# Graph message passing by sorting edges: smaller last copies in the sort's rotations, a split activation behind it, other zero matmuls ahead of it

## The chip, the cores and the metric

The kernel runs on one NeuronCore of a Trainium2 chip. The metric is the device time of one execution in microseconds (us); lower is better. Engines are named as in the profile: PE (matrix engine; PEld is its weight load), DVE (vector engine), ACT (scalar engine), POOL and SP (here mostly queues that issue transfers). A line number such as L1104 is a line of the kernel file before the change.

## The reference

There are N = 4096 nodes with D = 256 features and E = 262144 edges with random ends.

```python
self_out = nodes @ w_self
src_feat = nodes[edges_src]
msg = src_feat @ w_msg
agg = np.zeros((N, D), dtype=np.float32)
np.add.at(agg, edges_dst, msg)
return (self_out + agg).astype(np.float32)
```

## The kernel before

The kernel sorts the edges and then turns gather and scatter into dense matmuls. The order of instructions on every engine is written out by hand (`tc.manual_schedule()`), so each engine works its list strictly in the order of the program, and waits are placed by the data.

**Keys and the first sort.** Source and destination of each edge become one fp32 key in `XA` (128 partitions, 2048 columns). `_Sort.run` (L1109) walks over the list `SORT_A`. Entries 'b' are compare passes along the columns (a min and a max by DVE, all recorded at line L974). Entries 'q' are rotations: `rotate` (L1091) turns each column by its own number of partitions. There are eight rotations here, which the texts call the first to the eighth. The block `bb` of their columns is 32, 16, 8, 2, 2, 2, 1 and 2: in the seventh neighbouring columns belong to different turns, and a copy writes with a stride of 8 columns.

**A rotation** has two halves of 1024 columns. For each half PE multiplies eight groups of 128 columns by shifted identity matrices (fp32 matmuls, each recorded twice, so a half has 16 records at L1100). Four groups fill one PSUM tile `tp_sw` of 512 columns, of which there are four (`bufs=4`), and ACT copies each tile back to the other one of the two `XA` buffers (L1104), so a half has two copies.

**What lies between rotations.** `near` (L1028) does the passes up to the next rotation in waves: first what needs only the first half of the columns, then what completes the first half, then the second half. So PE can turn the first half while DVE still works on the second, and DVE can begin the next passes on the turned first half while PE turns the second.

**Zero matmuls.** `keep_warm(n)` (L991) issues n matmuls of zeros (128x512, tile `warm`, L994). `warm` (L978) places them ahead of a rotation's first half: for each number in `spans` it goes back that many us over DVE's compare operations, by estimated durations, and makes n zero matmuls wait for the operation found there. `WARM` (L48) lists spans and n for the eight rotations and the place behind the last of them. They stand in PE's list behind the second half of the rotation before, and ahead of the next rotation's matmuls. `FILLS` (L49) says how much of the dense work on the nodes (L321, L325) stands behind each rotation; behind the fourth, sixth and seventh there is none.

**Behind the rotations.** `relayout` (L1149) transposes the keys into `XS` and `XR`, `tail` (L1168) finishes the sort of the first half of the edges, with zero matmuls of its own ahead of its end. Then 16 fp32 matmuls (L453) and 16 more that subtract each chunk's base (L462) fill two PSUM tiles. ACT turns each tile into `vals` (int16, 1024 columns) with one Relu activation of 512 columns (L467): column 8q + k of `vals` comes from column 128k + q of the tiles, so any run of 8 columns needs both tiles. `split_vals` (L529) reads the first 32 columns of `vals` first (L536, L537), then columns 32 to 151, and so on.

**The main part.** For each of 2048 chunks of 128 edges, DVE and ACT build one-hot matrices (L579, L564, L592, L601), PE counts them into a ring in PSUM (L628), ACT moves finished runs to `atr` (L655), and PE multiplies those with the projected nodes `Y` (L718, L725). Group after group of chunks goes through two sets of one-hot buffers.

## Time and profile before

| | |
|---|---|
| median of 3 runs | 419.08 us (418.66 to 419.38) |
| the profiled execution | 418.17 us |
| its span, first to last instruction | 416.4 us |
| mean granted clock of PE over the span | 0.978 of full speed |
| busy: PE, DVE, ACT, POOL | 335.5, 374.9, 270.0, 43.0 us |

The span is split by the profile into work of engines and waits between them; 418.17 - 416.4 = 1.77 us of the profiled time lie outside it. The sort fills the span up to about 154 us, the main part the rest. [...] A row of the timeline merges like instructions in a row; its first number is the start, its second the time from the first start to the last end, and in brackets stands how long the engine sat idle before and what released it.

### The profile page before, as it was taken

Reading aid. Unit: us, or ns where it says so; the run is one execution under the profiler, and the core shown is the slowest. Engines: PE = TensorE matmul, PEld = TensorE weight load, DVE = VectorE, ACT = ScalarE, POOL = GpSimd, SP = SyncE. Lnnn points to the kernel's source line nnn. Section 1 sums busy time; section 2 is a strip of 40 time slices with the busy share of each in tenths; the row PEclk is TensorE's granted clock in tenths of the full one; section 3 lists DMA queues with packets and bytes.
Section 4 is the critical chain, followed back from the end, with each engine's and each line's share of the span. In section 5 each row is a group of like instructions: output and inputs, shape, how many; then the busy total and the mean of one; then the engine's idle time right before and its main releaser. Section 6 shows DMA issues by size and latency. Waiting matters only on the chain.

```text
span 416.4 us, 10756 instructions
## 1 busy us (share of the span) xinstructions
PE 335.5 (81%) x4128; PEld 287.9 (69%) x4137; DVE 374.9 (90%) x916; ACT 270.0 (65%) x559; POOL 43.0 (10%) x172
## 2 busy tenths in 40 slices
PE   0038477876967198999999998898988999999995
PEld 0025255564845056999999998797878988898895
DVE  6999999999799989999999999989997999998851
ACT  4328154553538015889888888996876877777782
POOL 8400000000000000002011020100102030202010
PEclk9999699999999689999999999999999999999999
DMA  8690000101023200003012020230203020211212
GB/s 305 138 185 4 2 1 2 50 0 52 1 101 116 87 0 2 2 2 39 2 16 28 2 32 10 53 41 8 33 3 39 2 32 12 28 14 15 29 16 53
DMA packets 18074, 16.20 MB, mean 39 GB/s; under 512 B 3684, under 2 KB 16997, under 8 KB 18022
## 3 DMA queue, kind: packets, MB, share of 16 engines
q0 software_dynamic: 8992, 6.29, 12.7%
q1 hardware_dynamic: 8310, 7.20, 5.3%
q10 hardware_dynamic: 720, 2.00, 1.2%
q8 instruction: 34, 0.56, 0.6%
q14 instruction: 18, 0.15, 0.1%
HBM read 8.93 MB, written 8.66 MB: 42 GB/s over the span
## 4 chain that ended last, share of the span: by engine, by line
DVE 47%; PE 45%; issue 3%; ACT 3%; DMA 1%; DVEq 0%; ACTq 0%
DVE XA L974 18%; PE out_ps L718 18%; PE ring L628 17%; DVE e_oh L601 7%; PE tp_sw L1100 5%; DVE d_oh L601 5%; DVE XS L974 4%; DVE XR L974 3%; DVE off L564 3%; PE warm L994 2%; PE out_ps L725 1%; DMA d<-in_edges_dst_dram 1%; ACT XA L1104 1%; DVE atr L688 1%; ACT atr L655 1%
## 5 line engine op out<-in xcount | busy, mean ns | idle before, releaser
L655 ACT CAST atr<-ring 128x472 bf16<-128x472 f32 (+11 forms) x352 | 177.2, 553 | 45.7 <-PE ring L628 40.7
L718 PE MATMUL out_ps<-Y,atr 128*128 128x256 bf16 x1024 | 162.2, 272 | 2.9 <-DVE atr L688 2.0
L628 PE MATMUL ring<-d_oh,e_oh 128*128 128x88 bf16 (+9 forms) x2048 | 149.7, 203 | 9.9 <-issue 4.5
L628 PEld LDWEIGHTS <-e_oh 128*128 128x128 bf16 x2048 | 129.2, 97 | 16.4 <-issue 9.7
L718 PEld LDWEIGHTS <-atr 128*128 128x128 bf16 x1024 | 90.7, 97 | 10.8 <-DVE atr L688 2.3
L974 DVE TENSOR_TENSOR XA<-XA 128x510 f32<-128x510 f32 (+30 forms) x154 | 89.3, 630 | 6.9 <-ACT XA L1104 5.3
L601 DVE TENSOR_SCALAR e_oh<-off 128x1024 bf16<-128x1024 int16 (+5 forms) x254 | 87.0, 402 | 7.9 <-PE ring L628 5.2
L628 PE MATMUL ring<-zer 128*128 128x158 bf16 (+12 forms) x352 | 81.4, 231 | 0.1
L866 POOL DMA_DIRECT2D out_dram<-o_sb x30 | 28.9, 963 | 357.8 <-ACT atr L655 357.8
L601 DVE TENSOR_SCALAR d_oh<-off 128x1024 bf16<-128x1024 int16 (+5 forms) x204 | 63.9, 373 | 0.0
L1104 ACT COPY XA<-tp_sw 128x512 f32<-128x512 f32 x32 | 20.9, 654 | 41.5 <-PE tp_sw L1100 41.2
L1100 PE MATMUL tp_sw<-XA,id 128*128 128x128 f32 x256 | 36.7, 298 | 7.9 <-DVE XA L974 7.8
L1100 PEld LDWEIGHTS tp_sw<-XA,id 128*128 128x128 f32 x256 | 33.1, 194 | 13.7 <-DVE XA L974 8.7
L564 DVE TENSOR_TENSOR off<-pair,rows 128x2048 int16<-128x2048 int16 (+5 forms) x34 | 38.6, 1134 | 0.3
L628 PEld LDWEIGHTS <-zer 128*128 128x128 bf16 x352 | 34.1, 97 | 5.0 <-ACT atr L655 1.9
L994 PE MATMUL warm<-zw 128*128 128x512 bf16 x61 | 20.8, 440 | 17.5 <-DVE XS L974 9.3
L349 PE MATMUL x_ps<-id_bf,nodes_bf 128*128 128x128 bf16 x64 | 8.5, 304 | 29.3 <-DMA nodes_bf<-in_nodes_dram 28.0
L725 PE MATMUL out_ps<-Y,atr 128*88 128x256 bf16 (+7 forms) x115 | 31.2, 272 | 0.0
L688 DVE TENSOR_TENSOR atr<-atr 128x178 bf16<-128x178 bf16 (+24 forms) x100 | 23.7, 260 | 6.4 <-ACT atr L655 6.0
L349 PEld LDWEIGHTS <-nodes_bf 128*128 128x128 bf16 x64 | 6.6, 139 | 30.9 <-DMA nodes_bf<-in_nodes_dram 28.3
L321 PE MATMUL y_ps<-wcat,XT 128*128 128x256 bf16 x128 | 21.7, 278 | 6.9 <-ACT Y L325 2.8
L592 ACT ACTIVATE e_oh<-off,onesc 128x512 bf16<-128x512 uint16 (+5 forms) x36 | 24.6, 686 | 2.7 <-DVE off L564 2.7
(114 smaller groups left out, 223.3 us busy)
## 6 DMA issues: line engine op xcount, KB each, us to landing
out_dram<-o_sb POOLq DMA_DIRECT2D x30, 128.0 KB, 3.2
nodes_bf<-in_nodes_dram POOLq DMA_DIRECT2D x2, 1024.0 KB, 12.6
out_dram<-nodes_bf SPq DMA_DIRECT2D x4, 512.0 KB, 2.9
out_dram<-XA SPq DMA_DIRECT2D x4, 512.0 KB, 3.0
d<-in_edges_dst_dram SPq DMA_DIRECT2D x2, 512.0 KB, 5.5
s<-in_edges_src_dram ACTq DMA_DIRECT2D x2, 512.0 KB, 5.7
d<-in_edges_dst_dram SPq DMA_DIRECT2D x1, 480.0 KB, 9.6
s<-in_edges_src_dram ACTq DMA_DIRECT2D x1, 480.0 KB
```

Source lines behind the costliest of these rows:

```text
L564: tt(out=v[:, 0:n // 2].rearrange("p g w (k i) -> p (g w) k i", i=2), in0=pair[:, g].rearrange("p g w i -> p (g w) i").unsqueeze(2).to_bro ...
L601: ins = tss(out=o[:, 0:n // 2, j:j + m].rearrange("p g k i -> p g (k i)"), in_=v[:, 0:n // 2, w, 0:2 * m], scalar=float((-j0 if w else ON_ ...
L628: mm = nc.tensor.matmul(out=ap, lhsT=lhsT, rhs=rhs, start=start, stop=True, skip_group_check=True,).ins
L655: ins = nc.scalar.copy(out=at[:, 0:n], in_=ring[:, b:b + n]).ins
L688: tt(out=atr[:, j:j + n, 0:m], in0=atr[:, j:j + n, 0:m], in1=atr[:, i:i + n, at:at + m], op=ALU.add,)
L718: nc.tensor.matmul(out=out_ps[:, i, :], lhsT=at[:, t * P:(t + 1) * P], rhs=Y[:, b, :], start=(b == 0 and not last and t % 2 == 0), stop=(b ...
L725: nc.tensor.matmul(out=out_ps[0:m, 0, :], lhsT=spill[:, c0:c0 + m], rhs=Y[:, b, :], start=False, stop=False, skip_group_check=True,)
L866: nc.gpsimd.dma_start(out=dst, in_=src, accum_op=ALU.add).ins,
L974: self.nc.vector.tensor_tensor(out=out, in0=in0, in1=in1, op=op),
L994: self.nc.tensor.matmul(out=w[:], lhsT=self.zw[:, 0:P], rhs=self.zw[:], start=True, stop=True).ins
L1100: self.nc.tensor.matmul(out=tp[:, g * P:(g + 1) * P], lhsT=self.turned(rots[8 * h + 4 * t + g]), rhs=sel(x)[:, 4 * t + g], start=True, sto ...
L1104: self.nc.scalar.copy(out=sel(y)[:, 4 * t:4 * t + 4], in_=tp[:].rearrange("p (g i b) -> p g i b", g=4, b=bb),)
```

## The change

1. `rotate` fills and copies three PSUM tiles per half: one of four groups (512 columns) and two of two groups (256 columns). The matmuls are the same; a rotation has 6 copies where it had 4, and 6 tiles of the four `tp` buffers.
2. `vals` is written by four activations where there were two: first the columns 0 to 31 from each of the two tiles (16 elements per partition each), then the rest from each (496 elements). All four stand behind the matmuls of both tiles.
3. `WARM` is changed. Ahead of the first rotation there are five sets of three zero matmuls, at 6.0, 4.8, 3.6, 2.4 and 1.2 us, where there were two sets at 2.7 and 1.4. Ahead of the fifth, seventh and eighth rotation there are two sets of three (2.7 and 1.4), where there was one (1.6). The others keep two sets at 2.7 and 1.4.

```diff
-WARM = [((2.7, 1.4), 3)] * 4 + [((1.6,), 3), ((2.7, 1.4), 3), ((1.6,), 3), ((1.6,), 3), ((2.7, 1.4), 3)]
+WARM = [((6.0, 4.8, 3.6, 2.4, 1.2), 3)] + [((2.7, 1.4), 3)] * 8
+TURNED = ((0, 4), (4, 2), (6, 2))
...
-        nc.scalar.activation(
-            out=vals[:].rearrange("p (q k) -> p q k", k=GP)[:, :, 4 * t:4 * t + 4],
-            in_=tp[:].rearrange("p (k q) -> p q k", k=4),
-            func=ACTF.Relu, scale=-1.0, bias=top[:],
-        )
+    for q in (slice(0, 32 // GP), slice(32 // GP, P)):
+        for t, tp in enumerate(tps):
+            nc.scalar.activation(
+                out=vals[:].rearrange("p (q k) -> p q k", k=GP)[:, q, 4 * t:4 * t + 4],
+                in_=tp[:].rearrange("p (k q) -> p q k", k=4)[:, q],
+                func=ACTF.Relu, scale=-1.0, bias=top[:],
+            )
...
-            for t in range(2):
-                tp = self.psum.tile([P, 512], FP32, name="tp_sw", tag="tp", bufs=4)
-                for g in range(4):
+            for g0, n in TURNED:
+                tp = self.psum.tile([P, 512], FP32, name="tp_sw", tag="tp", bufs=4)[:, 0:n * P]
+                for g in range(n):
                     self.nc.tensor.matmul(
-                        out=tp[:, g * P:(g + 1) * P], lhsT=self.turned(rots[8 * h + 4 * t + g]),
-                        rhs=sel(x)[:, 4 * t + g], start=True, stop=True,
+                        out=tp[:, g * P:(g + 1) * P], lhsT=self.turned(rots[8 * h + g0 + g]),
+                        rhs=sel(x)[:, g0 + g], start=True, stop=True,
                     )
                 self.nc.scalar.copy(
-                    out=sel(y)[:, 4 * t:4 * t + 4],
-                    in_=tp[:].rearrange("p (g i b) -> p g i b", g=4, b=bb),
+                    out=sel(y)[:, g0:g0 + n],
+                    in_=tp.rearrange("p (g i b) -> p g i b", g=n, b=bb),
                 )
```

## Rows read from the trace of the kernel before

**Rows 1.** The page: granted clock in 40 slices; share of the chain by engine.

```profile
PEclk9999699999999689999999999999999999999999
...
DVE 47%; PE 45%; issue 3%; ACT 3%; DMA 1%; DVEq 0%; ACTq 0%
```

**Rows 2.** The chain in order of time: start, us, what; first and second rotation.

```profile
49.63 2.29 PE tp_sw L1100 x16
...
60.63 2.07 PE tp_sw L1100 x16
```

**Rows 3.** Timeline of DVE, 52 to 126 us: compare passes behind the rotations.

```profile
52.57 10.52 DVE L974 TENSOR_TENSOR XA<-XA 128x511 f32<-128x511 f32 x16 [0.66 <-ACT XA L1104]
63.34 10.49 DVE L974 TENSOR_TENSOR XA<-XA 128x511 f32<-128x511 f32 x16 [0.25 <-ACT XA L1104]
...
93.12 7.84 DVE L974 TENSOR_TENSOR XA<-XA 128x515 f32<-128x515 f32 x12 [0.26 <-ACT XA L1104]
...
109.09 3.03 DVE L974 TENSOR_TENSOR XA<-XA 128x510 f32<-128x510 f32 x8 [2.28 <-ACT XA L1104]
112.82 5.14 DVE L974 TENSOR_TENSOR XA<-XA 128x510 f32<-128x510 f32 x8 [0.70 <-ACT XA L1104]
118.33 7.84 DVE L974 TENSOR_TENSOR XA<-XA 128x514 f32<-128x514 f32 x12 [0.36 <-ACT XA L1104]
```

**Rows 4.** Timeline of ACT at the second rotation.

```profile
62.72 0.59 ACT L1104 COPY XA<-tp_sw 128x512 f32<-128x512 f32 x1 [0.31 <-PE tp_sw L1100]
...
65.23 0.59 ACT L1104 COPY XA<-tp_sw 128x512 f32<-128x512 f32 x1 [0.31 <-PE tp_sw L1100]
65.71 0.66 ACT L325 CAST Y<-y_ps 128x256 bf16<-128x256 f32 x2
```

**Rows 5.** Instruction groups of ACT by shape: count, busy us, mean ns, idle before.

```profile
L325 ACT COPY XA<-y_ps 128x256 f32<-128x256 f32 x16 | 5.2, 380 | 1.5 <-PE y_ps L321 1.5
...
L498 ACT ACTIVATE rel_q<-XR,g7f 128x128 int16<-128x128 f32 x8 | 2.9, 404 | 0.0
...
L519 ACT ACTIVATION_READ_ACCUMULATOR XR<-vals,limit 128x1 f32 x1 | 0.2, 192 | 0.0
```

**Rows 6.** The tile tp_sw: shortest, median and longest ns of its copies.

```profile
L1104 ACT COPY XA<-tp_sw x32: 586/590/1107, 51.1 to 117.7; 128x512 f32<-128x512 f32 x32
```

**Rows 7.** Timeline of PE: zero matmuls ahead of the first rotation and in the tail.

```profile
47.08 2.56 PE L994 MATMUL warm<-zw 128*128 128x512 bf16 x5 [5.32 <-DVE XA L974]
...
144.51 5.12 PE L994 MATMUL warm<-zw 128*128 128x512 bf16 x11 [9.25 <-DVE XS L974]
```

**Rows 8.** Windows: stretch, length, busy of five engines, granted clock, DMA.

```profile
50.00:50.50 0.50, 0.50 (x5) 0.50 (x4) 0.50 (x2) 0.00 (x0) 0.00 (x0) 0.70 0.00 0
...
149.25:149.50 0.25, 0.25 (x3) 0.23 (x2) 0.25 (x1) 0.00 (x0) 0.00 (x0) 0.93 0.00 0
```

**Rows 9.** Timeline of PE ahead of the fifth, seventh and eighth rotation.

```profile
86.42 0.81 PE L994 MATMUL warm<-zw 128*128 128x512 bf16 x3
87.47 0.99 PE L1100 MATMUL tp_sw<-XA,id 128*128 128x128 f32 x6 [0.24 <-DVE XA L974]
...
102.91 0.81 PE L994 MATMUL warm<-zw 128*128 128x512 bf16 x3
104.01 0.91 PE L1100 MATMUL tp_sw<-XA,id 128*128 128x128 f32 x3 [0.30 <-DVE XA L974]
...
111.48 0.83 PE L994 MATMUL warm<-zw 128*128 128x512 bf16 x2
112.15 0.72 PE L1100 MATMUL tp_sw<-XA,id 128*128 128x128 f32 x5
```

**Rows 10.** Timeline at the end of the sort: the activations of vals, its first reader.

```profile
153.12 1.52 ACT L467 ACTIVATE vals<-tp_sw,top 128x512 int16<-128x512 f32 x2 [17.45 <-PE tp_sw L462]
...
154.67 0.18 DVE L536 TENSOR_SCALAR pair<-vals 128x32 int16<-128x32 int16 x1 [1.09 <-ACT vals L467]
```

**Rows 11.** Timeline of PE at the third group of chunks.

```profile
162.69 0.28 PE L628 MATMUL ring<-d_oh,e_oh 128*128 128x88 bf16 x3 [1.10 <-DVE d_oh L601]
```

## The prediction

> **What bounds the kernel now.** I began with the page. Its chain of waits is almost all DVE and PE [rows 1], so an edit counts only where it moves the point at which one of them hands over to the other. Next I read that chain in order of time through the sort. It goes from DVE to PE and back at every rotation: DVE's passes, 16 records of PE that turn a half, one copy by ACT, then DVE again [rows 2]. The timeline of DVE shows what each handover costs: DVE sits idle for a copy behind every rotation, 0.66 us at the first, 0.25 at the second (the third and fourth are like it, 0.24 each), 0.26 at the fifth, 2.28 and 0.70 at the seventh, 0.36 at the eighth [rows 3]. Behind 118.33 no further idle of DVE for a copy stands in that group; DVE runs on into the tail, and the next place that the change touches is `vals`, for which DVE waits 1.09 us [rows 10]. A gain is passed on where nothing else is late, and it can be no larger than the idle that it eats. That is the method: handover by handover.

> **Smaller last copies.** A copy of 512 columns takes 0.590 us [rows 6], one of 256 columns 0.380 [rows 5]. So the last copy of a half ends 0.21 us sooner, if ACT is free when PE has finished the last two groups. There are three copies in a row now. The gap between the first and the last copy of a half is 0.59 + 0.31 = 0.90 us [rows 4]; ACT must fit the first copy and the middle one into it. Without overlap that is 0.59 + 0.38 = 0.97, 0.07 too much, and with the pauses between instructions the gain is only about 0.1. But a copy at 65.23 that lasts 0.59 is followed by another at 65.71, 0.48 after its start [rows 4], and two of 256 columns take 0.66 together, not 0.76. With overlap the first two need 0.48 + 0.28 = 0.76 us, and the last starts as soon as PE is done. I take 0.21 and keep 0.1 as the other bound. In the seventh rotation the copy writes with a stride and takes 1.107 us [rows 6]; with the fixed part that 0.590 and 0.380 imply (0.17 us) half of its columns take 0.17 + 0.94 / 2 = 0.64, a gain of 0.47. The other bound is a plain half, 0.55.

> The PSUM tiles cost nothing: the fifth and sixth tile of a rotation reuse the buffers of its first and second, whose copies end before PE turns the second half's second tile, a half (2.07 us) later. If that cover were gone, PE would wait up to one copy, 0.59.

> **The first rotation.** Ahead of it PE had been idle for 5.32 us, and six zero matmuls (five recorded) took 2.56 us, 0.43 each [rows 7], which is the pace of 1.2 GHz; the clock came up inside the slice 50.0 to 50.5 (0.70 there [rows 8], so at 50.3). The half ended at 49.63 + 2.29 = 51.92, though DVE had released it before 49.5. At full clock a half takes 2.07 [rows 2] and would end at about 51.5, 0.4 sooner. The new zeros start some 6 us ahead of the half, near 43.4. In the two places where rows show the clock rise it took 50.3 - 47.08 = 3.2 us, and in the tail 149.3 - 144.51 = 4.8 us, of zeros [rows 7, 8]; either brings it to 2.4 GHz before 49.5. The sets come 1.2 us apart and three zeros take 1.28 us even at the low clock, so they do not pile up into the rotation. With the smaller copy 0.4 + 0.21 = 0.61 of the 0.66 us idle goes. DVE then needs the turned second half one wave (2.57 us, half of 5.14 [rows 3]) later, at about 54.5; PE starts that half at 51.91 and its copy ends at 51.91 + 2.07 + 0.02 + 0.38 = 54.4. So it just fits.

> **Second and third rotation.** 0.21 of 0.25 us each, 0.42 together. The second half's copy also ends 0.21 sooner, so no new wait takes its place.

> **Fourth and fifth, with three more zeros.** The fourth gives 0.21. But the zeros ahead of the fifth stand behind the fourth's second half on PE, and the rotation behind them. Three zeros push the eighth rotation from 111.48 to 112.15, so one costs 0.22 at full clock [rows 9]; six take 1.34. The fifth rotation then starts at 86.42 + 1.34 = 87.76, not 87.47, and its first half is copied at 87.76 + 2.07 + 0.02 + 0.38 = 90.23. DVE, which reached that point at 93.12 - 0.26 - 2.57 = 90.29, would now be there at 90.08 and waits. It continues at 90.25, ends its wave at 92.82, when the second half's copy is there, and not at 93.12. The two rotations give 0.30 in place of 0.42 or more.

> **Sixth to eighth.** Six zeros behind the sixth's second half: the seventh starts at 102.91 + 1.34 = 104.25, not 104.01, which uses up the sixth's gain and 0.24 more. PE turns both halves of the seventh without a pause, so its last copy ends 0.24 later and 0.47 sooner: DVE goes on at 112.59, not 112.82. Then the eighth: three more zeros (0.67) and the delay (0.24) put its first half at 113.06, its copy at 113.06 + 2.07 + 0.02 + 0.38 = 115.53, and DVE, ready at 112.59 + 2.57 = 115.16, waits until 115.55, one wave before 118.12. Before, that was 118.33: 0.21 are left of what the copies alone would give (0.21 + 0.47 + 0.21 = 0.89).

> **The values.** DVE's first read needs both tiles. Before, it waited for the second activation of 512 columns, from about 153.95 to 154.65 [rows 10]. Now it waits for one of 16 columns. The nearest rows are 0.404 us for 128 columns with a bias and 0.192 for a single column [rows 5]; I take 0.30. So DVE starts at 153.95 + 0.30 + 0.02 = 154.27, 0.40 sooner (bounds 0.29 and 0.51). The two long activations run on to about 155.5, and nothing but the read of columns 32 to 151, some 4 us later, needs them. At the third group of chunks PE waits 1.10 us for DVE's one-hots [rows 11], so PE takes over the whole shift there, and I see nothing in the main part tied to absolute time.

> [...]

> **Sum.** 0.61 + 0.42 + 0.30 + 0.21 + 0.40 = 1.94 us. Against its own time the profiled execution would come to 418.17 - 1.94 = 416.23 us. The median of the runs is 0.91 above that execution, and all three runs are. Carried along unchanged that gives 417.14. But part of the 0.91 can be the clock. Had it risen at the first rotation 4.8 us after the first zero, as in the tail, it would have risen at 51.9, 1.6 us later; at half speed that costs PE 0.8 us, all on the chain. The early zeros remove that in every execution. I split the difference and put the forecast at 416.6 us.

> [...]

> **Rivals.**
> (a) The copies do not overlap: 0.1 in place of 0.21 at seven handovers, about 0.5 less in all: 417.1. For it speaks that waits on PE lie between them; against it the row at 65.71.
> (b) The clock takes some back, or the runs' 0.91 us has another cause. The tail's zeros are unchanged and the rise came there at 149.3, just in time for its matmuls. Shifted by 1.6 us it would cost 0.8: 417.4, and 417.9 if the 0.91 stays too.
> (c) The gain is hidden: DVE finds the second half's copy late, so that only the first rotation's clock (0.4) and the values (0.4) count: 419.08 - 0.8 = 418.3, or 417.8 with half of the 0.91. Margins of 0.1 us at the first rotations speak for it.
> (d) Slower: the added zeros become the bound. At 0.43 each, six take 2.56. The fifth rotation starts 1.5 late and loses about 1.2. The seventh starts at 105.47, 1.46 late, and the eighth at 111.48 + 1.46 + 2.56 = 115.50, 3.35 late against a slack of 0.9: 2.5 lost. Against 1.43 gained elsewhere this is 2.3 slower, 420.9 counted from where the forecast starts (418.6). It decides from a clock of about 1.2 GHz between 84 and 118 us; the slices show 9 there throughout [rows 1].

> **How the numbers follow.** The forecast has 0.55 (its own range 416.0 to 417.2), (a) 0.15, (b) 0.14, (c) 0.08, (d) 0.04; 0.04 remain for no change. Leaving out the upper part of (b) and (c), (d), no change and the tails of the forecast, the range is 415.6 to 417.7. About 0.2% (0.84 us) is what a measurement of this kernel can tell from no change. Faster by more takes the forecast, (a), (b) and most of (c), 0.91; within it 0.05; slower 0.04.

> **What the profile of the changed kernel would show.** Granted clock 1.0 in the whole first rotation. DVE's idle below 0.1 us at the first four rotations; copies of about 0.38 us, the last of a half starting with no ACT work ahead of it. Six zeros directly in front of the fifth, seventh and eighth rotation, with no idle of PE, and DVE idle 0.2 and 0.4 us where it now waits for their first halves. DVE's first read of `vals` about 0.4 us behind the last L462 matmul. I am wrong if ACT's three copies stand end to end, if DVE's idle only moves to second halves, or if the clock falls ahead of a rotation.

## The result, and the profile after

The changed kernel takes 412.63 us (412.34 to 412.87, 4 runs) against 418.87 for the kernel before (418.18 to 419.38, 4 runs): a ratio of 0.9852, 95% interval 0.9835 to 0.9869. It is 6.24 us faster; the forecast was some 2.3 us, 416.6, and its range ended at 415.6.

The two profiled executions differ by 5.40 us (418.17 and 412.77; spans 416.4 and 411.0). I cut that at two events of the timeline of DVE: its first compare pass and its first read of `vals`.

```
us                              before   after   difference
start to the first pass          19.18   18.75     -0.43
sort: first pass to vals        135.49  134.21     -1.28
main part: vals to the end      261.73  258.04     -3.69
```

The first line is the loading of the data, which the change does not touch. The second holds everything that I priced, at 1.94. The third, the largest, is a part of the program in which no line was changed.

The page of after, clock and shares of the chain, answers to [rows 1]: the 6 in the fifth slice is gone (the rise ahead of the first rotation), and the dip at the tail is a little deeper (5 and 7 where it was 6 and 8).

```profile
PEclk9999999999999579999999999999999999999999
...
DVE 48%; PE 44%; ACT 3%; issue 3%; DMA 1%; DVEq 0%; ACTq 0%
```

The granted clock is given as a share of full speed, and the zero matmuls show the pace that goes with it. In before two of them from 47.08 take 1.06 us and one 0.63, so the next starts 0.43 us later, at a granted clock of 0.50; three from 58.84 take 0.81 and one 0.38, so 0.215 us each, at 1.00. For 512 columns that is 1.2 and 2.4 columns per ns, which the prediction writes as GHz. In after the zeros ahead of the first rotation start 0.43 us apart at 43.06 and 0.215 at 46.77, 2.3 us ahead of the half, though the profile gives 1.00 in both places.

The chain of after at the first rotation, in order of time, answers to [rows 2]. The half takes 2.06 us in place of 2.29, its last copy 0.38.

```profile
49.06 2.06 PE tp_sw L1103 x16
51.12 0.02 issue
51.15 0.38 ACT XA L1107
```

The timeline of DVE in after, start, length, instruction and idle time ahead of it, answers to [rows 3]. Through the first four rotations 63 passes follow each other without one idle time that is shown; before, there were 0.66 and three of about 0.25. From the fifth on four idle times stand.

```profile
49.50 39.12 DVE L977 TENSOR_TENSOR XA<-XA 128x487 f32<-128x487 f32 x63
88.87 16.00 DVE L977 TENSOR_TENSOR XA<-XA 128x511 f32<-128x511 f32 x28 [0.25 <-ACT XA L1107]
107.26 3.03 DVE L977 TENSOR_TENSOR XA<-XA 128x510 f32<-128x510 f32 x8 [2.39 <-ACT XA L1107]
110.98 2.62 DVE L977 TENSOR_TENSOR XA<-XA 128x510 f32<-128x510 f32 x4 [0.69 <-ACT XA L1107]
114.09 10.36 DVE L977 TENSOR_TENSOR XA<-XA 128x510 f32<-128x510 f32 x16 [0.49 <-ACT XA L1107]
```

The timeline of ACT in after: a third rotation's copies, one of the seventh's, and the small activation of `vals`. Answers to [rows 4], [rows 6] and [rows 10].

```profile
71.37 1.22 ACT L1107 COPY XA<-tp_sw 128x512 f32<-128x512 f32 x3 [2.88 <-PE tp_sw L1103]
...
106.61 0.62 ACT L1107 COPY XA<-tp_sw 128x256 f32<-128x256 f32 x1 [0.26 <-PE tp_sw L1103]
...
151.82 0.27 ACT L470 ACTIVATE vals<-tp_sw,top 128x16 int16<-128x16 f32 x1 [17.87 <-PE tp_sw L463]
```

Three copies (512, 256 and 256 columns) take 1.22 us with no idle time between them: 0.13 less than 0.59 + 0.38 + 0.38, so they overlap.

The timeline of PE in after, ahead of the seventh and the eighth rotation, answers to [rows 9]. Six zeros begin at 101.19 and the rotation at 102.70, 1.51 later: 0.25 for one, not the 0.22 of the forecast.

```profile
101.19 1.67 PE L997 MATMUL warm<-zw 128*128 128x512 bf16 x6
102.70 7.60 PE L1103 MATMUL tp_sw<-XA,id 128*128 128x128 f32 x32
110.36 1.46 PE L997 MATMUL warm<-zw 128*128 128x512 bf16 x5
111.65 1.95 PE L1103 MATMUL tp_sw<-XA,id 128*128 128x128 f32 x16
```

**The main part.** The groups of instructions of PE show where its time changed. First the kernel before, from 150 us on, then after, the same group: count, busy time, mean ns, idle time ahead of the group and what ended it. "issue" is idle time for which the profile names no releaser.

```profile
L628 PE MATMUL ring<-d_oh,e_oh 128*128 128x88 bf16 (+9 forms) x2048 | 149.7, 203 | 9.9 <-issue 4.5 <-DVE d_oh L601 2.3 <-DVE atr L688 1.1
```

```profile
L631 PE MATMUL ring<-d_oh,e_oh 128*128 128x88 bf16 (+9 forms) x2048 | 147.9, 203 | 5.7 <-issue 2.2 <-DVE d_oh L604 2.0 <-DVE off L567 0.2
```

The wait for DVE's `d_oh` is about the same. Of the 4.2 us by which this group's idle time is shorter, 2.3 had no releaser. Such an idle time looks like this, on the timeline of PE in the kernel before:

```profile
318.34 0.20 PE L628 MATMUL ring<-d_oh,e_oh 128*128 128x89 bf16 x1
319.76 0.30 PE L628 MATMUL ring<-d_oh,e_oh 128*128 128x89 bf16 x3 [1.23 <-issue]
...
299.44 0.33 PE L628 MATMUL ring<-d_oh,e_oh 128*128 128x85 bf16 x4
300.37 0.20 PE L628 MATMUL ring<-d_oh,e_oh 128*128 128x85 bf16 x1 [0.60 <-issue]
```

PE stops in the midst of a run of like matmuls, and the profile shows nothing that it waits for. The DMA view of the kernel before, 316 to 318 us, shows what else happened: a transfer of instructions near 317.05 (the lone 9; what follows it belongs to a store), 2.7 us ahead of the end of the stall at 319.76. The page counts 34 of them in after (`q8 instruction: 34, 0.56` MB), some 9 us apart in the main part.

```profile
DMA  0000000000000000000009000000009999599639
...
q8 instruction: 1, 0.02, 4.5%
```

### The profile page after: what moved, and what is told of

It is laid out like the page before. It is cut to its first block, busy times and chain, and to the rows that moved or that the text cites. A ratio compares the mean times of both kernels' runs of the same rounds, so it can differ in the third digit from the quotient of the medians.

```text
span 411.0 us, 10816 instructions
## 1 busy us (share of the span) xinstructions
PE 339.0 (82%) x4145; PEld 289.7 (70%) x4155; DVE 374.5 (91%) x916; ACT 270.3 (66%) x577; POOL 46.1 (11%) x172
## 4 chain that ended last, share of the span: by engine, by line
DVE 48%; PE 44%; ACT 3%; issue 3%; DMA 1%; DVEq 0%; ACTq 0%
DVE XA L977 19%; PE out_ps L721 18%; PE ring L631 17%; DVE e_oh L604 7%; DVE d_oh L604 5%; DVE XS L977 4%; PE tp_sw L1103 4%; DVE off L567 3%; DVE XR L977 3%; PE warm L997 2%; PE out_ps L728 2%; ACT XA L1107 2%; DMA d<-in_edges_dst_dram 1%; DVE atr L691 1%; DVE XA L260 1%
## 5 line engine op out<-in xcount | busy, mean ns | idle before, releaser
L631 PE MATMUL ring<-d_oh,e_oh 128*128 128x88 bf16 (+9 forms) x2048 | 147.9, 203 | 5.7 <-issue 2.2
L869 POOL DMA_DIRECT2D out_dram<-o_sb x30 | 32.2, 1072 | 349.5 <-ACT atr L658 349.5
L1107 ACT COPY XA<-tp_sw 128x256 f32<-128x256 f32 (+1 forms) x48 | 21.7, 492 | 38.4 <-PE tp_sw L1103 38.2
L997 PE MATMUL warm<-zw 128*128 128x512 bf16 x78 | 25.1, 432 | 14.4 <-DVE XS L977 9.3
L997 PEld LDWEIGHTS <-zw 128*128 128x128 bf16 x87 | 8.5, 105 | 27.7 <-DVE XS L977 9.6
```

Of the source, the lines that this page charges most:

```text
L631: mm = nc.tensor.matmul(out=ap, lhsT=lhsT, rhs=rhs, start=start, stop=True, skip_group_check=True,).ins
L869: nc.gpsimd.dma_start(out=dst, in_=src, accum_op=ALU.add).ins,
L997: self.nc.tensor.matmul(out=w[:], lhsT=self.zw[:, 0:P], rhs=self.zw[:], start=True, stop=True).ins
L1107: self.nc.scalar.copy(out=sel(y)[:, g0:g0 + n], in_=tp.rearrange("p (g i b) -> p g i b", g=n, b=bb),)
```

## The experiments

The **offset** of a kernel is the number of PE instructions added ahead of the main part, modulo 256; before has 0, after 36. Up to e16 the text counts weight loads and matmuls alone; with PE's own waits some kernels lie one further or one less, as said behind e16 and in the table. "Tiny zeros" are zero matmuls of 32 x 32 in an idle time of PE ahead of the tail, of two instructions each: the page of e1, with 18, counts 4146 matmuls and 4155 weight loads, before's 4128 and 4137. The idle time there is 9.3 us in before and in after; 8.3 are left with 18 of them (e1) and 6.1 with 110 (e4). An added instruction makes a cut fall earlier in the main part; the expectations of e8, e10, e11, e12 say "later" for that, with the right amounts. The times of before are those of the same chip, and each ratio has its 95% interval.

### Moving the cuts and nothing else

```diff
+    pad = psum_sort.tile([P, 512], FP32, name="warm", tag="warm", bufs=1)
+    for _ in range(18):
+        nc.tensor.matmul(out=pad[0:32, 0:32], lhsT=zw[:, 0:32], rhs=zw[:, 0:32], start=True, stop=True)
     own = sort.tail(XS, plan, halo)
```

e1 is the kernel before with this. e2 is the kernel after with the `WARM` line of before, e3 the kernel before with the `WARM` line of after, e4 the kernel after with 110 tiny zeros (36 + 220 = 256 instructions).

> The kernel before, with 18 tiny zero matmuls more on PE (32 columns, 36 instructions with their weight loads) in PE's 9 us of idle time ahead of the tail's zero matmuls; nothing waits for them. Theory A (the main part's time hangs on where PE's instruction stream is cut into blocks of 256, and the stalls of PE marked as issue stand at the cuts): the cuts fall in the main part where the changed kernel has them, so its stretch from the third group of chunks to the end takes 250.0 us and not 253.7, and the time is 418.9 - 3.7 = 415.2. Rival B (the main part is faster because the sort ends earlier or otherwise, so that the engines and the stores meet differently): no change, 418.9.

> The changed kernel with the zero matmuls of the kernel before (the smaller last copies and the split activation stay). As many PE instructions ahead of the main part as before. Theory A: the main part takes 253.7 us as before, and only the sort's gain is left: 0.21 at each of the first to fifth, the sixth and the eighth rotation, 0.47 at the seventh, 0.4 at the values, about 2.3 us in all, 416.5. Rival B: the main part takes about 250 us, 412.5 or a little less.

> The kernel before with the zero matmuls of the changed kernel alone. Theory A: the main part is at 250.0 us as in the changed kernel (-3.7), the first rotation gains 0.4 and the zeros ahead of the fifth, seventh and eighth rotation cost up to 1.2, so about 415.5. Rival B: the main part stays at 253.7, 418.5 to 419.7.

> The changed kernel with 110 tiny zero matmuls more (32 columns, 220 instructions) in PE's idle time ahead of the tail's zero matmuls: with the change's own 36 that makes 256, so the cuts fall in the main part where the kernel before has them. Theory A: the stretch from the third group of chunks to the end is back at 253.7 us and the time at about 412.6 + 3.7 = 416.3. Rival B: 412.6.

Measured, with before at 418.75: e1 415.61 (0.9947, 0.9917 to 0.9978), e2 418.47 (0.9996, 0.9979 to 1.0013), e3 415.67 (0.9915, 0.9885 to 0.9946), e4 418.39 (0.9986, 0.9967 to 1.0005). Eighteen matmuls that compute nothing and touch nothing make the kernel before 3.1 us faster by the medians (2.2 by the ratio of all runs, 0.9 to 3.5), without a gain in the sort; with 110 in the changed kernel, 256 added instructions in all, its gain is gone (e4). The cuts' place is worth about as much as all that the change was priced at, or more. In the same group of e1 the stalls without a releaser are down from 4.5 to 1.3 us, and stand at other chunks than before. (Others stand ahead of other groups; over the whole main part they fall from 4.7 to 3.8.)

```profile
L631 PE MATMUL ring<-d_oh,e_oh 128*128 128x88 bf16 (+9 forms) x2048 | 148.1, 203 | 5.1 <-DVE d_oh L604 2.1 <-issue 1.3 <-DVE e_oh L604 0.2
```

But e2 and e4 came out 2 us above what the theory gave: their sorts are shorter than before's (133.5 and 134.1 us against 135.5), yet the time shows no gain. In e4 the stalls of this group have grown to 8.3 us:

```profile
L634 PE MATMUL ring<-d_oh,e_oh 128*128 128x88 bf16 (+9 forms) x2048 | 149.5, 203 | 12.9 <-issue 8.3 <-DVE d_oh L607 2.9 <-DVE off L570 0.2
```

### The parts of the change at one place of the cuts

e5 is e2 with the 18 tiny zeros. e6 keeps the five sets ahead of the first rotation and has before's zeros elsewhere, with nine tiny ones; e7 is the kernel before with the split activations of `vals` and 18 tiny ones. All have offset 36. e8 is the kernel after with 46 tiny zeros (offset 128).

```diff
-WARM = [((6.0, 4.8, 3.6, 2.4, 1.2), 3)] + [((2.7, 1.4), 3)] * 8
+WARM = [((6.0, 4.8, 3.6, 2.4, 1.2), 3)] + [((2.7, 1.4), 3)] * 3 + [((1.6,), 3), ((2.7, 1.4), 3), ((1.6,), 3), ((1.6,), 3), ((2.7, 1.4), 3)]
```

> The kernel after with the zero matmuls of before, and 18 tiny zero matmuls ahead of the tail that put the cuts of PE's stream into blocks of 256 instructions where they lie in the kernel after. It differs from e2_old_zeros (418.47 us) by the 18 tiny matmuls alone. A (the places of the cuts make the main part long or short): 412.5 to 414, the main part about 258. B (the smaller copies themselves lengthen the main part when the zeros are the old ones): 417.5 to 418.5, as e2_old_zeros.

> The kernel after with five sets of zeros ahead of the first rotation but the zeros of before ahead of all others (nine fewer), and nine tiny zeros ahead of the tail, so that the cuts lie as in the kernel after. A (the second sets ahead of the fifth, seventh and eighth rotation cost the sort about 0.3 us in all and the main part does not notice): 412.2 to 412.4, sort 133.9. B (they cost nothing, or warm the clock): 412.6 or more.

> The kernel before with the values' activations split as in the change, and 18 tiny zeros that put the cuts where they lie in the kernel after; it differs from e1_before_pad18 (415.61 us) by the values alone. A (the sort's gain reaches the end once the cuts stay where they are): 0.40 us under e1_before_pad18, 415.2. B (a shift of the main part is eaten by its stalls, or brings more than itself): no gain, 415.6, or a fall of more than 1 us.

> The kernel after with 46 tiny zeros ahead of the tail: its cuts lie 92 instructions later than in the kernel after, 128 (half a block) from those of before. A (what a cut costs depends on what it falls on, and before's place is a bad one): some time between 411.5 and 417, with stalls of PE at other chunks than in either kernel. B (any padding that isn't 36 modulo 256 brings the long main part): 417.5 to 418.5.

Measured, with before at 419.10: e5 412.72 (0.9840, 0.9807 to 0.9874), e6 411.18 (0.9798, 0.9763 to 0.9833), e7 415.83 (0.9930, 0.9888 to 0.9972), e8 418.92 (0.9982, 0.9954 to 1.0011). e5 and e2 differ by 18 tiny matmuls and by 5.7 us. e8 has the changed kernel's whole sort and none of its gain; its time lies above the ranges of both theories. The 0.40 us of `vals` cannot be seen in e7: its runs lie between 413.6 and 420.7.

e6 is the fastest kernel of the study, below the changed kernel, and by more than the 0.3 us expected. The timeline of its DVE shows where:

```profile
49.39 55.81 DVE L980 TENSOR_TENSOR XA<-XA 128x487 f32<-128x487 f32 x92
107.03 3.04 DVE L980 TENSOR_TENSOR XA<-XA 128x510 f32<-128x510 f32 x8 [1.82 <-ACT XA L1110]
110.75 13.14 DVE L980 TENSOR_TENSOR XA<-XA 128x510 f32<-128x510 f32 x20 [0.69 <-ACT XA L1110]
```

The idle times shown are 1.82 + 0.69 = 2.51 us, after's 0.25 + 2.39 + 0.69 + 0.49 = 3.82. The timeline merges over idle times below 0.15 us, of which e6 has more. Counted from the first pass, DVE stands behind the eighth rotation 2.32 us earlier than before in e6 and 1.27 in after, so the second sets of zeros ahead of the fifth, seventh and eighth rotation cost the sort 1.05 us; they stand on PE in front of work for which DVE waits.

### Where in the block, and whether the stores do it

e9 is the kernel before without its 30 adding stores. e10, e11 and e12 are e6 with 0, 27 and 87 tiny zeros (offsets 18, 72 and 192).

```diff
-                    tc.add_manual_dep(
-                        nc.gpsimd.dma_start(out=dst, in_=src, accum_op=ALU.add).ins,
-                        evac_of[nev].name, DEP, reason="pace",
-                    )
```

> The kernel before without its 30 adding stores of the sums (so the output lacks them); instructions of PE and cuts as before. A (the transfer that brings the next block is late because the stores' packets share the DMA engines with it): the stalls at the cuts go, main part 258 or less, time 415 or less. B (the transfer is late by itself, however free the engines are): the same stalls at the same chunks, some 4.5 us in all, main part 260 to 262, time 417 to 419.

> e6_five_sets_only (411.18 us) without its nine tiny zeros: the cuts lie 18 instructions later than before's and 18 earlier than after's. A (what a cut costs goes by where it falls in the stretch, so near places cost alike): between 411 and 414. B (only after's place is short, any other is long): 416.5 to 417.5. C (before's place reaches this far): 416.5 to 417.5 too.

> e6_five_sets_only with 27 tiny zeros instead of nine: the cuts lie 72 instructions later than before's, 36 later than after's. A: between 411 and 414.5. B (only after's place is short): 416.5 to 417.5.

> e6_five_sets_only with 87 tiny zeros: the cuts lie 192 instructions later than before's, 64 earlier in the next block. A: between 413 and 417. B (only after's place is short): 416.5 to 417.5.

Measured, with before at 418.44: e9 417.27 (0.9975, 0.9946 to 1.0005), e10 413.46 (0.9903, 0.9867 to 0.9939), e11 413.74 (0.9885, 0.9823 to 0.9947), e12 417.13 (0.9969, 0.9944 to 0.9994). Without the stores the stalls stay, 4.2 us in the place of 4.5, so the stores' packets are not what makes the stalls:

```profile
L628 PE MATMUL ring<-d_oh,e_oh 128*128 128x88 bf16 (+9 forms) x2048 | 149.6, 203 | 9.4 <-issue 4.2 <-DVE d_oh L601 2.6 <-DVE atr L688 1.1
```

Offsets 18 and 72 are short like 36, offset 192 is long like 0 and 128: near places cost alike. Theory A held for e10 and e11; e12 ended 0.13 us above its range, and inside that of B.

### Why the sort's gain is lost at before's cuts

e13, e14 and e15 are e2, the kernel after and the kernel before with the reduction ahead of the tail's bases made three times, which writes the same values and was to start the main part 2.44 us later. e16 is the kernel before with the smaller copies alone.

```diff
+        for _ in range(2 if h == 0 else 0):
+            nc.vector.tensor_reduce(out=k16[:, z], in_=_view3(own, P), axis=AX.X, op=ALU.min)
```

> e2_old_zeros (418.47 us; cuts as before) with the reduction ahead of the tail's bases made three times in place of once, which starts the main part 2.44 us later. A (with the cuts of before PE's stalls take up a shift of the start, which is why the sort's gain vanished in e2_old_zeros): 418.3 to 419.3. B (the start is passed on, and the smaller copies or the split values lengthen the main part themselves): 420.5 to 421.3.

> The kernel after with the same two added reductions; its cuts stay. A and B both (with after's cuts a shift of the start reaches the end): 414.7 to 415.5. If it stays at 412.6 to 413.5, the stalls take up a shift here too.

> The kernel before with the same two added reductions. A (stalls take up the shift): 418.5 to 419.8. B (it is passed on): 420.8 to 421.6.

> The kernel before with the smaller last copies alone; values, zeros and cuts as before. The sort is about 1.3 us shorter. A (stalls take up the shift): 418.2 to 419. B (what lengthened the main part of e2_old_zeros are the split values): 417.0 to 417.7.

Measured, with before at 419.55: e13 422.20 (1.0048, 1.0023 to 1.0074), e14 416.76 (0.9929, 0.9900 to 0.9958), e15 421.38 (1.0043, 1.0027 to 1.0059), e16 418.97 (0.9987, 0.9963 to 1.0011). The later start reaches the end at either place of the cuts: by the ratios 2.2 us against e2, 3.2 against after, 1.8 against before. My theory A, that the stalls take up a shift, is refuted for the whole of it: e13 and e14 lie above all ranges, e15 in that of B. That a part is taken up is not excluded. Counted from the first pass, the main part starts 3.6 us later in the profiled executions of e13 and e14 than in those of e2 and after, and not 2.44, among other things because the granted clock fell to half once more, at 154.0 and 152.3 us: the 16 matmuls that subtract the bases take 2.72 and 3.48 us there, 2.05 in e15. In e15 it starts 2.3 later than in before.

In e16 there are no split activations, its sort is 1.84 us shorter (133.65 us against 135.49), and the gain is 0.58; its time lies in the range of A, whose cause e13 to e15 do not bear out. I took this to mean that the smaller copies lengthen the main part by themselves. The runs do not show that, for two reasons.

First, e16's cuts are not before's. With tiles of two groups a matmul of the eighth rotation has to wait both for its buffer (ACT) and for its data (DVE), and the second wait is an instruction of its own. The trace holds it, at the line of the rotation's matmuls, first before, then e16 (x8 and x9 are the counts):

```profile
L1100 PEldq EVENT_SEMAPHORE  x8: 51/51/51, 87.4 to 115.5; - x8
...
L1101 PEldq EVENT_SEMAPHORE  x9: 51/51/51, 86.4 to 113.6; - x9
```

All kernels with the smaller copies have this wait, so e2, e4, e13 and e16 have offset 1 and not 0, and after 37; e3 has one wait less than before, offset 35. The stalls follow: counted from the main part's first matmul they stand at 4651 and 6699 in before, at 4649 and 6697 in e2, e4, e13 and e16 (each matmul has a weight load ahead of it, so a step of one can show as two).

Second, in e16's profiled execution PE waited 1.73 us for DVE ahead of 284.83, and behind it the granted clock was half (in the second row stand the stretch, its length, the busy time of PE, of its weight loads, of DVE, ACT and POOL, the granted clock and the DMA):

```profile
284.83 0.20 PE L629 MATMUL ring<-d_oh,e_oh 128*128 128x85 bf16 x1 [1.73 <-DVE d_oh L602]
...
286.00:288.00 2.00, 2.00 (x19) 1.54 (x17) 1.99 (x7) 1.60 (x3) 0.59 (x1) 0.50 0.00 0
```

Compared matmul by matmul from the first read of `vals`, e16 is 0.30 us behind before ahead of this stretch, 1.66 behind it and 1.83 at the end. Most of its longer main part is this stretch, in this execution. e4 has no such stretch and is 2.73 behind at the end.

One trace was left when I planned the last two runs: stalls of the kernels with smaller copies stand a little earlier than before's, though the list of the main part is the same. e17 is the kernel before with one tiny zero (offset 2), e18 is e16 with 127 (offset 254).

> The kernel before with one tiny zero matmul ahead of the tail: each cut falls two instructions earlier in the main part. The stalls of the kernels with smaller copies and before's cuts stand one chunk earlier than before's own (at 1143, 1216 and 1814 in place of 1144, 1217 and 1815), as if their stream held an instruction or two more than the listing shows. A (such a small step of the cuts is what lengthens their main part): main part 264 to 266 and stalls at the chunks of e16_copies_only, time 420 to 422. B (the copies lengthen it in another way): main part 261 to 262.5, time as before.

> e16_copies_only with 127 tiny zeros (254 instructions, two short of a block), which puts each cut two instructions later in the main part than in e16_copies_only. A: main part 261 to 262.5 and stalls at before's chunks, time 416 to 417.5. B: main part 264 to 265, time as e16_copies_only, 418.5 to 419.5.

Measured, with before at 418.88: e17 419.32 (1.0018, 0.9997 to 1.0039), e18 416.99 (0.9959, 0.9933 to 0.9984). The stalls moved as A said: e17 has them at 4649 and 6697, as e16, and e18 at 4651 and 6699, as before. e18 gained the sort's time back, as A expected; e17 rose by 0.44 us where A asked for more than 1, and cannot be told from no change. The one profiled execution of each has a main part that lies nearest B (260.9 and 264.0), and a time off the median of its kernel, 417.45 and 418.95; that of e18 has a stretch at half the clock too (twelve matmuls of `out_ps` take 2.57 us from 286.98 on, in before 1.47), across which it loses 1.6 us against before. With the wait counted, e18 lies at 255 and e17 at 2. So offset 1 with the smaller copies loses the sort's gain, and 255 keeps it. A step of an instruction or two may explain the loss in e2, e4, e13 and e16; but no run has the smaller copies at offset 0, or the old ones at offset 1, and it is not settled.

All kernels in one table: offset with PE's own waits counted, main part and stalls without a releaser (of 0.15 us or more) in the profiled execution, and the ratio to before.

```
offset  kernels            main part us             stalls us         ratio
0       before             261.7                    4.7               1
0       e9 e15             261.2 262.4              4.9 6.1           0.998 1.004
1       e2 e4 e13 e16      266.3 264.5 264.9 264.2  7.6 9.4 8.9 6.5   1.000 0.999 1.005 0.999
2       e17                260.9                    5.9               1.002
255     e18                264.0                    3.7               0.996
19      e10                259.0                    5.2               0.990
35      e3                 259.6                    3.4               0.992
36      e1 e7              258.2 258.8              3.8 3.8           0.995 0.993
37      after e5 e6 e14    258.0 256.9 257.5 256.3  3.3 2.6 1.4 1.7   0.985 0.984 0.980 0.993
73      e11                260.3                    5.0               0.989
129     e8                 263.8                    9.7               0.998
193     e12                264.2                    9.0               0.997
```

The main part is short at offsets 19 to 73 (256.3 to 260.3 us) and longer at the others (260.9 to 266.3). The stalls do not make up the whole of that: from before to after they fall by 1.4 us of 3.7, from before to e1 by 0.9 of 3.5. That the place of the cuts sets the time is shown by the padded runs; that it does so through these stalls alone is not shown.

## Why the prediction was wrong

The direction was right; the time was not, and the range did not hold it. The step that failed is the last of the part on the values: "PE takes over the whole shift there, and I see nothing in the main part tied to absolute time". The shift was taken over as said: the wait at the third group of chunks is 1.09 us in after where [rows 11] has 1.10. But the same sentence lets the main part keep its length, and it became 3.69 us shorter. What changed it, as e1, e5 and e4 show, is the count of PE instructions ahead of it, and I had priced the added zeros by their time on PE alone. "The PSUM tiles cost nothing" has the same gap: they cost one wait instruction. None of my rivals had a main part that changes.

At one place of the cuts the changed copies, values and zeros are worth 412.63 against 415.61 in e1, 3.0 us (the sort of e1's profiled execution is 2.46 us longer than after's, its main part 0.16); the cuts are worth 3.1 by the medians and 2.2 by the ratio (e1 against before). So about half of the 6.24 us is the change itself, and the rest the place to which it happened to push the main part: luck, as far as the forecast goes.

Going through the terms of the sum:

- **First rotation**, 0.61: DVE is 0.59 us earlier behind it, counted from the first pass. The half ran at the full clock.
- **The clock there**, for which the forecast took off some 0.5 of the 0.91 us: right in kind. In the ten other profiled executions with the old zeros ahead of the first rotation DVE stands behind it between 0.18 us earlier and 1.15 later than in before (e1, where a rotation's matmul takes 304 ns in the mean, 298 in before); in the nine with the five sets it is 0.37 to 0.59 earlier in all. So this pair of executions shows less of the sort's gain than most pairs would.
- **Second to fourth**, 0.21 each: 0.21, 0.22 and 0.22. The copies overlap, and rival (a) falls. e16, with the copies alone, gains 1.74 us from the second rotation to the eighth where the same terms give 1.73.
- **Fifth and sixth**: together with those ahead of them 1.51 us where the sum had 1.54.
- **Seventh and eighth**, mis-sized: the sum had 1.54 in all behind the eighth; 1.27 were left. Six zeros take 1.51 us, not 1.34; two such sets, 0.17 each, are enough for the missing 0.27. DVE waited 0.69 us for the seventh's second half, as before, and 0.49 at the eighth, where the sum had 0.39. I had priced the second sets at some 0.8 us against the copies alone; e6 shows 1.05.
- **Values**, 0.40: the small activation takes 0.27 us (0.30 forecast), yet DVE waits 1.09 us as before. The cause is the clock. In after it came up behind the start of the tail's transposes (147.92), and these took 2.27 us (1.95 before), which ate the gain; in e6 it came up ahead of them (0.81 from 146 to 147, 1.00 from 147 on), they took 2.01, and DVE waits 0.66 us, 0.43 less. In e2, e4, e5, e10, e11 and e12 it waits 0.66 to 0.68 too, so the 0.40 holds in most executions. What after shows is the part of rival (b) that came true in this execution.

The windows of after show half speed to 148 and the rise behind it; below them stand the transposes, of after and of e6:

```profile
147.00:148.00 1.00, 1.00 (x4) 0.56 (x3) 0.97 (x4) 0.00 (x0) 0.00 (x0) 0.50 0.00 0
148.00:149.00 1.00, 1.00 (x8) 1.00 (x7) 0.97 (x2) 0.00 (x0) 0.00 (x0) 0.71 0.00 0
...
147.92 2.27 PE L454 MATMUL tp_sw<-ident,XS 128*128 128x128 f32 x16
...
146.88 2.01 PE L457 MATMUL tp_sw<-ident,XS 128*128 128x128 f32 x16
```

The cuts I did not weigh at all: 126 of the 127 stalls stand at places 242 to 250 modulo 256, and PE's stalls without a releaser add up to between 1.4 us (e14) and 9.7 us (e8) of the main part.

**What stays open.** Why PE stalls at some cuts and not at others: the stores are ruled out by e9. What the rest of the shorter main part is, which the stalls do not make up. And whether the smaller copies lose the sort's gain at offset 1 by that one instruction or in another way. With profiles of one execution each and runs that spread over 3 to 7 us at some places, I could not tell.

## What to carry to other kernels

Before you price an edit to a long unrolled program, count the instructions that it adds on PE, and ask what lies behind them: here 36 bring 2 to 3 us in a part that the edit does not touch. A tile that has to wait for two engines added an instruction too (9 waits at the rotations' matmuls in e16, 8 in before). Test a small gain at several offsets, by padding with instructions that do nothing, before you credit it to the edit; an edit that "made no difference" may have been paid for by the cuts (e2, e4, e8). And put work that fills a pause only where the engine has nothing queued behind it: the second sets of zeros in this change cost the sort 1.05 us, and leaving them out gave the fastest kernel, 411.18 us.

## What I had not expected of the hardware

- How long one such stall can be: 1.85 us in e1, just ahead of 318.29, in a main part that is instruction for instruction that of before, where none is over 1.23.
- TensorE's clock fell in the main part of some executions. In e2's profiled execution PE was idle for 1.74 us ahead of 284.22, and the granted clock from 286 to 288 was 0.51, half speed; that execution, 420.21 us, is the slowest of its kernel. The main parts of e16 and e18 have such a stretch behind the same matmul, after PE had waited 1.73 and 1.85 us for DVE: e16's granted clock was 0.50 from 286 to 288, and twelve matmuls behind it take 2.60 us in e16 and 2.57 in e18, 1.47 in before. A comparison of main parts has to look for it first.
